# Columns of weights taken two abreast at the start of each group of products, in a hybrid RWKV-7 and neighbourhood-attention trunk on one core

## The chip, the cores and the metric

The kernel runs on one core of one Trainium2 chip. Its time is the device time of one execution in microseconds (us); a comparison takes the median of several runs. PE is the tensor engine, DVE the vector engine, ACT the scalar engine, POOL GpSimd, SP the engine that issues most DMAs. Each engine works through its own queue strictly in the order in which the program wrote it: an instruction that waits holds up everything behind it on its engine.

## The reference

Two requests of 512 tokens by 1024 features pass through two layers with shared weights. Layer 0 is RWKV-7 time mixing with a forward and a backward scan; layer 1 is neighbourhood attention on a grid. Cut to what matters here:

```python
xx = 0.5 * (x_prev + x_next) - xn
lerp = lambda j: xn + xx * mu[j]
r = heads(lerp(0) @ w_r); k = heads(lerp(1) @ w_k); v = heads(lerp(2) @ w_v)
z = xn @ w_z
...                       # decay, a, kk from small products of lerp(3..6)
s = s * w_t + sa b_t + v_t k_t ;  y_t = s r_t      # scan over t, for both directions
out = norm(y) * silu(z);  h = out @ w_o;  x = x + rms_norm(h)
proj = rms_norm(x) @ w_in + b_in                   # layer 1: q, k, v, z
...                       # attention in 8 x 16 windows, gate, w_o, norm, residual
```

All of it is float32. A large product is made of three passes in a faster rounded format: both factors are split into a high and a low half, and high x high, high x low and low x high are added up in one PSUM bank.

## The kernel before, in words

A *column* is 128 output features of one weight matrix: 24 matmuls of 128x512, three for each of eight slices k of the 1024 input features (`gemm`, L430 to L432; in the scan `products`, L826 to L828). A column needs its weights, two halves of 512 wide, each fetched (`raw`), cast to the high half on ACT (`whi`, L379 or L745) and subtracted to the low half on DVE (`wlo`, L380 or L747). It also needs the operands x of its group: eight pairs of tiles `act`, again a cast on ACT (L379 or L771) and a subtraction on DVE (L380 or L773). All columns of one matrix and one request share the operands and form a *group*.

**Before the scan** the work is written as ordinary code and a list scheduler sets the order of each engine. The columns of z for request 0 (z0 to z7) are followed by those of k (k0 to k7). They accumulate in the two PSUM banks called `zy`. A finished z column is taken out of its bank by DVE (L643), a finished k column by ACT (L657, L666). The work on request 1 (`prelude(1)`) runs alongside: squares of x summed on DVE (L445), a sum over features on PE (L458), a square root on ACT (L463), a reciprocal and a diagonal matrix on DVE (L465, L468), its spread on PE (L472). The products L565 to L567 of the small decay matrices follow, and L670 sums the squares of a finished k column.

**In the scan** there are 64 steps in eight blocks of eight: a block is a pair of column groups of one request. A planner (`weave`) writes the queues of PE, DVE and ACT itself, from estimated costs. It holds a set of threads: the scan's steps (first in rank), `preps` and `inverse`, which prepare a block's small matrices, `finish` for its end, and `flow`, which works off nine groups of columns as fill: r and v of request 0, k, r, v and six columns of z of request 1, w_o of request 0, the last two columns of z, then 24 columns of w_in (its operands are made by DVE from the end of layer 0, L795 and L797). Products have the last rank: they fill the time in which PE waits for the scan. Where the planner sees PE idle and cooling down, it writes a filler matmul into a spare bank (L1643). The banks are: two for `pf`, one for `us`, two for `zy`, and three for `pm`. The three `pm` banks hold the columns in work, the columns that wait to be taken out (`posts`), and the small products of `preps` (L896 and L897, taken out by ACT at L900), `inverse` (L1049, L1051), `finish` (L1302, L1312) and the transposes of v (L704, taken out by L707).

Weights live in four pairs of half-column buffers (`NW`), raw weights in three, operands in eighteen `act` tiles, that is nine pairs for groups that need eight. So the next group's operands can be made only as the current group's last column gives its own up, one by one.

**After the scan** (w_o, attention, the second request's w_in) nothing of this applies.

Of the kernel before, what the change touches and what calls it, by code (L numbers as in the profile page):

```python
# [19 lines left out]
P = 128  # L20
# [3 lines left out]
NP = 8  # L24
# [207 lines left out]
class Trunk:  # L232
# [10 lines left out]
    LAST = ("pg", "pg", "po", "pm")  # L243
    PG, PT, NK, NPT = 2, 2, 2, 3
    AHEAD, AHEADW, SCAN_A, SCAN_W = 0, 0, 300, 300
    NAB, NX, NR, NY, NSB, NBI = 2, 2, 2, 2, 4, 2
# [385 lines left out]
    def column(self, s, kind, p, ps):  # L632
# [29 lines left out]
        if kind == "k":  # L662
# [15 lines left out]
            if p == NP - 1:  # L678
                yield "S", None, lambda c: c.at([sp["ss", s].tensor.name])
# [33 lines left out]

    def columns(self, s, kind, x, ps=range(NP)):
        for p in ps:
            w = self.first.pop() if self.first else self.weight(self.a["w_" + kind][p])
            ps = yield from self.gemm(w, x, self.gt)
            for _ in self.column(s, kind, p, ps):
                pass
            yield  # L720

    def flow(self):
# [8 lines left out]
        for k, t in enumerate(self.groups[0][1]):  # L731
            x[0, k] = t

        def loads():
            for c, (_, _, src, _) in enumerate(cols):
                for j in range(2):
                    yield "S", lambda: did["load"] < did["split"] + self.NRAW
                    raw[2 * c + j] = self.load(self.t("raw", (P, self.WP), self.NRAW), src[:, j * self.WP:(j + 1) * self.WP])
                    did["load"] += 1

        def splits():
            for h in range(2 * len(cols)):
                yield "A", lambda: h < did["load"] and h < did["k"] // 4 + self.NW, lambda c: c.at(name(raw[h]))
                hi, lo = (self.t(tag, (P, self.WP), self.NW, F32R) for tag in ("whi", "wlo"))
# [69 lines left out]
        def products():  # L814
            free, room = self.bank()
            for c, (g, j, _, done) in enumerate(cols):
                for k in range(KT):
                    h = 2 * c + k // 4
                    at = slice(k % 4 * P, k % 4 * P + P)
                    yield (  # L820
                        "P", lambda: h in w and (g, k) in x and (k > 0 or (free() and c - 2 not in self.post)),
                        lambda c: max(c.at(name(*w[h], *x[g, k])), 0.0 if k else room(c)))
                    if k == 0:
                        ps = self.p("pm")
                    (hi, lo), (xh, xl) = w[h], x[g, k]
                    nc.tensor.matmul(ps, hi[:, at], xh, start=(k == 0), stop=False)  # L826
                    nc.tensor.matmul(ps, hi[:, at], xl, start=False, stop=False)  # L827
                    nc.tensor.matmul(ps, lo[:, at], xh, start=False, stop=(k == KT - 1))  # L828
                    did["k"] += 1
                    if j == len(self.groups[g][2]) - 1:  # L830
                        did["x"] += 1
                self.post[c] = done(ps)

        def posts(a):
            for c in range(a, len(cols), 2):
# [491 lines left out]
    def out0s(self, s, p, ps):  # L1327
# [14 lines left out]
        else:  # L1342
# [3 lines left out]
            nc.vector.tensor_tensor(self.h_acc, sq, self.h_acc, op=ALU.add)  # L1346
        if p == NP - 1:
            self.made.add(("h", s))
# [309 lines left out]
    def scan_phase(self, mid):  # L1658
# [27 lines left out]
        def fetch():  # L1686
            for q in qs:
                st = self.steps[q]
                yield (
                    "S", lambda: did["states"] >= q - 1 and did["preps"] > st.n and ("v", st.s, 2 * st.pb + 1) in self.made,  # L1690
                    lambda c: c.at([self.sp["ab", st.s, st.pb].tensor.name]))
# [22 lines left out]
        def finish():  # L1714
            for n, (s, pb) in enumerate(self.todo):
                yield "S", lambda: did["steps"] >= NCH * (n + 1) and ("z", s, 2 * pb + 1) in self.sp
                yield from self.finish(s, pb, self.steps[NCH * n].y)
# [16 lines left out]
    def run(self):  # L1734
# [74 lines left out]
class Step:  # L1809
# [122 lines left out]
```

## Time and profile before

| what | value |
|---|---|
| median of 3 runs | 1655.09 us (1649.51 to 1655.29) |
| profiled execution, its own time | 1656.04 us |
| its span in the profile | 1654.2 us |
| PE, DVE, ACT busy | 1558.4, 1220.0, 1014.5 us |
| mean granted PE clock | 0.977 |
| first and last product of the scan's `flow` (L826) | 168.3 and 1159.6 us |

The profiled execution took 0.95 us more than the median, and 1.84 us more than its span. Matmuls overlap in the pipeline: a 128x512 matmul is shown for 0.39 us while the next starts 0.23 us after it, so PE's busy time counts some of it twice where it is dense. A wait in brackets behind a row is the idle time of the engine before that instruction, with what ended it.

### The profile page before, as it was taken

What the parts mean: (1) busy time and instruction counts of PE and PEld (TensorE: products, weight loads), DVE (VectorE), ACT (ScalarE), POOL (GpSimd) and SP (SyncE); (2) the same over time, 40 slices, a digit from 0 to 9 for tenths busy, and PEclk for the clock granted to TensorE, in tenths of its full rate; (3) what the DMA queues carried; (4) which work ended last, traced back from release to release, by engine and by line L of the source; (5) the groups of instructions that cost most, each with busy time, mean ns of one, the idle gap of its engine ahead of it and who ended that gap; (6) DMA issues with size and microseconds to landing.
All of it is one profiled execution on the core that took longest, in us unless ns stands there. A gap on an engine that the chain in (4) does not pass through costs nothing.

```text
span 1654.2 us, 46534 instructions
## 1 busy us (share of the span) xinstructions
PE 1558.4 (94%) x18826; PEld 1195.2 (72%) x18826; DVE 1220.0 (74%) x2711; ACT 1014.5 (61%) x2027; POOL 178.2 (11%) x338
## 2 busy tenths in 40 slices
PE   7989899898989998999888999999999999999998
PEld 6867667676767776766666777777777788777776
DVE  8886669588778786897788897855576685665564
ACT  6577655766755767566475665454567665455562
POOL 0000213311101133100000011000000002100000
PEclk9989999899999999999997999999999999999999
DMA  6455678666677687675776674554864346745553
GB/s 212 158 176 185 183 270 279 217 227 227 206 246 255 201 279 261 201 252 165 226 229 225 199 255 166 179 190 127 276 222 164 109 140 213 244 157 175 169 159 107
DMA packets 176184, 336.29 MB, mean 203 GB/s; under 512 B 20928, under 2 KB 53824, under 8 KB 175968
## 3 DMA queue, kind: packets, MB, share of 16 engines
q1 hardware_dynamic: 152480, 253.07, 47.7%
q0 software_dynamic: 23488, 80.23, 13.8%
q8 instruction: 148, 2.42, 0.6%
q14 instruction: 68, 0.56, 0.1%
HBM read 227.71 MB, written 105.51 MB: 201 GB/s over the span
## 4 chain that ended last, share of the span: by engine, by line
PE 48%; DVE 7%; ACT 5%; DMA 3%; issue 3%; POOL 0%; SPq 0%; DVEq 0%; ACTq 0%; POOLq 0%
PE pg L430 6%; PE pg L431 6%; PE pg L432 6%; PE pm L826 4%; PE pm L827 3%; PE pm L828 3%; PE pf L1114 2%; PE sc L1452 2%; PE po L1485 2%; PE pt L1470 2%; PE us L1233 1%; PE zy L1186 1%; PE us L1213 1%; PE zy L1237 1%; DMA v<-dv 1%
## 5 line engine op out<-in xcount | busy, mean ns | idle before, releaser
L826 PE MATMUL pm<-act,whi 128*128 128x512 f32 x640 | 283.9, 444 | 7.8 <-ACT act L795 3.2
L827 PE MATMUL pm<-act,whi 128*128 128x512 f32 x640 | 257.2, 402 | 10.8 <-DVE act L773 10.1
L828 PE MATMUL pm<-act,wlo 128*128 128x512 f32 x640 | 256.2, 400 | 5.5 <-DVE wlo L747 5.5
L430 PE MATMUL pg<-act,whi 128*128 128x512 f32 x384 | 158.4, 412 | 0.4 <-DVE tmp L1408 0.4
L826 PEld LDWEIGHTS pm<-act,whi 128*128 128x128 f32 x640 | 121.7, 190 | 50.9 <-issue 10.7
L379 ACT CAST whi<-raw 128x512 fp32r<-128x512 f32 x148 | 91.4, 617 | 107.7 <-PE pg L431 66.1
L432 PE MATMUL pg<-act,wlo 128*128 128x512 f32 x384 | 152.5, 397 | 0.0
L431 PE MATMUL pg<-act,whi 128*128 128x512 f32 x384 | 152.4, 397 | 0.0
L827 PEld LDWEIGHTS pm<-act,whi 128*128 128x128 f32 x640 | 122.8, 192 | 36.7 <-DVE act L773 15.9
L828 PEld LDWEIGHTS pm<-act,wlo 128*128 128x128 f32 x640 | 122.7, 192 | 35.5 <-DVE wlo L747 8.9
L380 DVE TENSOR_TENSOR wlo<-raw,whi 128x512 fp32r<-128x512 f32 x148 | 101.3, 686 | 61.1 <-ACT whi L379 60.3
L747 DVE TENSOR_TENSOR wlo<-raw,whi 128x512 fp32r<-128x512 f32 x160 | 108.9, 683 | 33.3 <-ACT whi L745 33.1
L745 ACT CAST whi<-raw 128x512 fp32r<-128x512 f32 x160 | 97.8, 617 | 44.6 <-PE pm L827 23.3
L430 PEld LDWEIGHTS pg<-act,whi 128*128 128x128 f32 x384 | 72.2, 188 | 15.5 <-issue 3.3
L432 PEld LDWEIGHTS pg<-act,wlo 128*128 128x128 f32 x384 | 72.2, 188 | 14.9 <-issue 0.3
L431 PEld LDWEIGHTS pg<-act,whi 128*128 128x128 f32 x384 | 72.4, 189 | 14.1 <-issue 2.5
L1018 DVE TENSOR_TENSOR etmp<-N 128x30 f32<-128x30 f32 (+14 forms) x240 | 78.4, 327 | 4.3
L1020 DVE TENSOR_TENSOR N<-etmp,N 128x30 f32<-128x30 f32 (+14 forms) x240 | 78.5, 327 | 4.0
L1463 DVE CUSTOM_DVE_ANT_0 sb<-sc,bias 128x256 f32<-128x256 f32 x128 | 49.2, 418 | 26.2 <-PE pt L1470 20.1
L1466 ACT ACTIVATE sb<-sb,mx 128x256 f32<-128x256 f32 x128 | 64.1, 502 | 6.9 <-DVE mx L1465 6.6
L1114 PE MATMUL pf<-cab 64*64 64x128 f32 (+1 forms) x2048 | 67.0, 268 | 0.3 <-PE zy L1092 0.3
L1137 DVE TENSOR_TENSOR AK<-zy,cc 128x256 f32<-128x256 f32 x63 | 26.6, 422 | 53.0 <-PE zy L1092 52.5
(409 smaller groups left out, 3686.8 us busy)
## 6 DMA issues: line engine op xcount, KB each, us to landing
dab<-ab POOLq DMA_DIRECT2D x32, 1024.0 KB, 7.0
cab<-dab SPq DMA_DIRECT2D x64, 512.0 KB, 5.0
raw<-in_w_in_dram SPq DMA_DIRECT2D x128, 256.0 KB, 2.9
bias<-in_rpb_dram SPq DMA_DIRECT2D x32, 384.0 KB, 5.2
raw<-in_w_z_dram SPq DMA_DIRECT2D x32, 256.0 KB, 3.6
raw<-in_w_k_dram SPq DMA_DIRECT2D x32, 256.0 KB, 3.0
raw<-in_w_r_dram SPq DMA_DIRECT2D x32, 256.0 KB, 4.2
k<-dk SPq DMA_DIRECT2D x32, 256.0 KB, 4.6
```

The lines of the kernel that those rows point to most:

```text
L379: self.nc.scalar.copy(hi, src)
L380: (eng or self.nc.vector).tensor_tensor(lo, src, hi.bitcast(F32), op=ALU.subtract)
L430: nc.tensor.matmul(ps, hi, x[k][0], start=(k == 0), stop=False)
L431: nc.tensor.matmul(ps, hi, x[k][1], start=False, stop=False)
L432: self.mm = nc.tensor.matmul(ps, lo, x[k][0], start=False, stop=(k == KT - 1))
L745: nc.scalar.copy(hi, raw[h])
L747: nc.vector.tensor_tensor(lo, raw.pop(h), hi.bitcast(F32), op=ALU.subtract)
L826: nc.tensor.matmul(ps, hi[:, at], xh, start=(k == 0), stop=False)
L827: nc.tensor.matmul(ps, hi[:, at], xl, start=False, stop=False)
L828: nc.tensor.matmul(ps, lo[:, at], xh, start=False, stop=(k == KT - 1))
L1020: vt.tensor_tensor(N[:, q + 1:, :q], tv, N[:, q + 1:, :q], op=ALU.add)
L1114: end = nc.tensor.matmul(st.f[half(a), h, 0, d, g] if st.last else st.f[half(a), h, :, d, g], ab[half(h), d, g, 2 * e[d] + 1 - a], rt if s ...
```

## The change

In the scan, the first two columns of every group except the first (`PAIRS`) are worked abreast: slice k of the one, slice k of the other, then slice k + 1. Each operand that arrives now serves six matmuls at once. The order of loads and splits of weight halves follows the order of use, and a buffer is free again when its half has been used four times. The ends of columns are worked by three threads in place of two, so a pair's two ends can be open beside a third. The last two columns (`ENDS`) could be paired too; that list is empty. Since ends may come out of order now, four gates wait for all of a set of tiles in place of the last one. Before the scan, z6 and z7 are written as a pair, and k0 and k1.

```diff
+    PAIRS, ENDS = (1,2,3,4,5,6,7,8), ()
...
-    def columns(self, s, kind, x, ps=range(NP)):
+    def columns(self, s, kind, x, ps=range(NP), two=()):
         for p in ps:
-            w = self.first.pop() if self.first else self.weight(self.a["w_" + kind][p])
-            ps = yield from self.gemm(w, x, self.gt)
-            for _ in self.column(s, kind, p, ps):
-                pass
-            yield
+            if p - 1 in two:
+                continue
+            pair = (p, p + 1) if p in two else (p,)
+            made = [self.gemm(self.first.pop() if self.first else self.weight(self.a["w_" + kind][q]), x, self.gt) for q in pair]
+            outs = yield from abreast(made)
+            for q, ps in zip(pair, outs):
+                for _ in self.column(s, kind, q, ps):
+                    pass
+                yield
...
+            two = [a for a, gs in ((0, self.PAIRS), (n - 2, self.ENDS)) if g in gs]
+            if j in two:
+                turns += [(c + e, k) for k in range(KT) for e in range(2)]
+            elif j - 1 not in two:
+                turns += [(c, k) for k in range(KT)]
+        halves = [2 * c + k // 4 for c, k in turns if k % 4 == 0]
...
-                yield "A", lambda: h < did["load"] and h < did["k"] // 4 + self.NW, lambda c: c.at(name(raw[h]))
+                yield "A", lambda: n < did["load"] and (n < self.NW or used[halves[n - self.NW]] == 4), lambda c: c.at(name(raw[h]))
...
-            for c, (g, j, _, done) in enumerate(cols):
-                for k in range(KT):
+            for c, k in turns:
...
-                        "P", lambda: h in w and (g, k) in x and (k > 0 or (free() and c - 2 not in self.post)),
+                    "P", lambda: h in w and (g, k) in x and (k > 0 or (free() and c - 3 not in self.post)),
...
-            Thread(lambda: 9, products()), Thread(lambda: 2, posts(0)), Thread(lambda: 2, posts(1))]
+            Thread(lambda: 9, products()), *(Thread(lambda: 2, posts(a)) for a in range(3))]
...
-        run(self.columns(0, "z", self.xz), (a, 1))
-        run(self.columns(0, "k", self.shifted(0, 1)), (a, 1))
+        run(self.columns(0, "z", self.xz, two=(6,)), (a, 1))
+        run(self.columns(0, "k", self.shifted(0, 1), two=(0,)), (a, 1))
...
+def abreast(gens):
+    out = [None] * len(gens)
+    todo = list(enumerate(gens))
+    while todo:
+        for n, g in list(todo):
+            try:
+                next(g)
+            except StopIteration as end:
+                out[n] = end.value
+                todo.remove((n, g))
+                continue
+            yield
+    return out
```

How the instructions stand is shown at three places. In the order of the changed kernel the line numbers are shifted: L431 to L433 are the old L430 to L432, L459 and L473 the old L458 and L472, L644 the old L643, L845 to L847 the old L826 to L828, L1665 the old L1643.

First, PE's queue at the join of z and k before the scan. Before, z7 (zy_836) is followed at once by k0 (zy_970):

```order
L430 MATMUL zy_836<-act_140,whi_832 128x512
L431 MATMUL zy_836<-act_139,whi_832 128x512
L432 MATMUL zy_836<-act_140,wlo_833 128x512
L430 MATMUL zy_970<-act_906,whi_962 128x512
L431 MATMUL zy_970<-act_905,whi_962 128x512
L432 MATMUL zy_970<-act_906,wlo_963 128x512
```

Now (z6 is zy_749, z7 is zy_758, k0 is zy_982):

```order
L433 MATMUL zy_749<-act_140,wlo_734 128x512
L431 MATMUL zy_758<-act_140,whi_745 128x512
L432 MATMUL zy_758<-act_139,whi_745 128x512
L433 MATMUL zy_758<-act_140,wlo_746 128x512
L459 MATMUL pm_849<-ones,acc_786 128x1 x4
L473 MATMUL pm_862<-tmp_857,ones 128x128 x4
L431 MATMUL zy_982<-act_906,whi_962 128x512
L432 MATMUL zy_982<-act_905,whi_962 128x512
```

The norm's two small products of request 1, which stood inside and behind k0, now stand ahead of it. The scheduler left z6 all but one matmul ahead of z7, and k0 wholly ahead of k1: the pairs written there are hardly abreast in the queue.

Second, DVE's queue where z6 is taken out of its bank. Before (zy_737 is z6) it is the 115th row of the queue, in the middle of the norm's sums:

```order
L380 TENSOR_TENSOR wlo_963<-raw_958,whi_962 128x512
L445 TENSOR_TENSOR acc_773<-tmp_806,acc_773 128x512
L643 TENSOR_TENSOR tmp_812<-zy_737,vs_158 128x512
L584 SCALAR_TENSOR_TENSOR lm_650<-lr_651,lm_650 128x512
L380 TENSOR_TENSOR wlo_967<-raw_960,whi_966 128x512
```

Now (zy_749 is z6, zy_758 z7) it is the 137th, behind the norm's reciprocal and diagonal; z7's follows as the 142nd, where before it was the 145th:

```order
L466 RECIPROCAL rs_854<-rs_854 128x4
L617 SCALAR_TENSOR_TENSOR xr_951<-xx_415,dv,xr_951 128x512
L469 TENSOR_SCALAR tmp_857<-cc,rs_854 128x128 x4
L644 TENSOR_TENSOR tmp_886<-zy_749,vs_158 128x512
L617 SCALAR_TENSOR_TENSOR xr_1668<-xx_360,dv,xr_1668 128x512
L612 TENSOR_TENSOR h_138_667<-lr_651,h_138_667 64x512
L617 SCALAR_TENSOR_TENSOR xr_1675<-xx_372,dv,xr_1675 128x512
L381 TENSOR_TENSOR act_954<-xr_951,act_955 128x512
L644 TENSOR_TENSOR tmp_894<-zy_758,vs_158 128x512
```

The bank that k0 needs is free only after that row.

Third, PE's queue in the scan at the start of the last group (w_in), ahead of the sixth block. Before, one column (pm_12277) starts, with fillers (L1643) and the inverse's products (L1049) between its slices:

```order
L826 MATMUL pm_12277<-act_12240,whi_12170 128x512
L827 MATMUL pm_12277<-act_12239,whi_12170 128x512
L828 MATMUL pm_12277<-act_12240,wlo_12171 128x512
L1643 MATMUL zy_11763<-cc 128x256
L1049 MATMUL pm_12289<-NA_12254,Go_8993 32x32 x32
L1643 MATMUL zy_11763<-cc 128x256 x3
```

Now two columns (pm_12263 and pm_12274) stand abreast:

```order
L1665 MATMUL zy_11824<-cc 128x256 x5
L845 MATMUL pm_12263<-act_12256,whi_12150 128x512
L846 MATMUL pm_12263<-act_12255,whi_12150 128x512
L847 MATMUL pm_12263<-act_12256,wlo_12151 128x512
L845 MATMUL pm_12274<-act_12256,whi_12192 128x512
L846 MATMUL pm_12274<-act_12255,whi_12192 128x512
L847 MATMUL pm_12274<-act_12256,wlo_12193 128x512
L1665 MATMUL zy_11824<-cc 128x256 x8
L845 MATMUL pm_12263<-act_12300,whi_12150 128x512
```

Each operand serves two columns, and there are more fillers at this place than before. Over the whole program the fillers are 101 before and 103 now. No other count of instructions changes but ACT's loads of its function table, which fall by two. From the last steps of the scan to the end, all queues read alike.

More of the change, by code (lines that the diff above doesn't have):

```diff
@@ L678, in column @@
             if p == NP - 1:
-                yield "S", None, lambda c: c.at([sp["ss", s].tensor.name])
+                yield "S", lambda: all(("k", s, q) in self.made for q in range(NP)), lambda c: c.at([sp["ss", s].tensor.name])
                 rn = self.tmp((P, 64))
@@ L815, in products @@
             free, room = self.bank()
[L816 to L832 removed]
+            out = {}
+            for c, k in turns:
+                g, j, _, done = cols[c]
+                h = 2 * c + k // 4
+                at = slice(k % 4 * P, k % 4 * P + P)
+                yield (
+                    "P", lambda: h in w and (g, k) in x and (k > 0 or (free() and c - 3 not in self.post)),
+                    lambda c: max(c.at(name(*w[h], *x[g, k])), 0.0 if k else room(c)))
+                if k == 0:
+                    out[c] = self.p("pm")
+                ps = out[c]
+                (hi, lo), (xh, xl) = w[h], x[g, k]
+                nc.tensor.matmul(ps, hi[:, at], xh, start=(k == 0), stop=False)
+                nc.tensor.matmul(ps, hi[:, at], xl, start=False, stop=False)
+                nc.tensor.matmul(ps, lo[:, at], xh, start=False, stop=(k == KT - 1))
+                did["k"] += 1
+                used[h] += 1
+                if j == len(self.groups[g][2]) - 1:
+                    did["x"] += 1
+                if k == KT - 1:
+                    self.post[c] = done(out.pop(c))
         def posts(a):
[L835 removed]
+            for c in range(a, len(cols), 3):
                 yield "A", lambda: c in self.post
@@ L1689, in fetch @@
                 yield (
-                    "S", lambda: did["states"] >= q - 1 and did["preps"] > st.n and ("v", st.s, 2 * st.pb + 1) in self.made,
+                    "S", lambda: did["states"] >= q - 1 and did["preps"] > st.n and all(("v", st.s, 2 * st.pb + g) in self.made for g in range(2)),
                     lambda c: c.at([self.sp["ab", st.s, st.pb].tensor.name]))
@@ L1715, in finish @@
             for n, (s, pb) in enumerate(self.todo):
-                yield "S", lambda: did["steps"] >= NCH * (n + 1) and ("z", s, 2 * pb + 1) in self.sp
+                yield "S", lambda: did["steps"] >= NCH * (n + 1) and all(("z", s, 2 * pb + g) in self.sp for g in range(2))
                 yield from self.finish(s, pb, self.steps[NCH * n].y)
```

20 lines of the change are left out of this document (13 added, 7 removed).

## The prediction

> **What bounds the kernel now.** I read the page's first two parts, then the stretches of time, then PE's waits inside the scan, and last the order of time at the join of z and k.
>
> ```profile
> span 1654.2 us, 46534 instructions
> ...
> PE 1558.4 (94%) x18826; PEld 1195.2 (72%) x18826; DVE 1220.0 (74%) x2711; ACT 1014.5 (61%) x2027; POOL 178.2 (11%) x338
> ...
> core 0: us, PE busy (x) PEld busy (x) DVE busy (x) ACT busy (x) POOL busy (x), PEclk, DMA share, GB/s
> 62.00:84.00 22.00, 21.00 (x94) 17.05 (x92) 20.84 (x34) 16.72 (x30) 0.24 (x4) 1.00 0.34 115
> 84.00:96.00 12.00, 8.77 (x29) 6.48 (x29) 11.84 (x23) 10.52 (x17) 0.02 (x1) 0.57 0.18 54
> 96.00:142.00 46.00, 46.00 (x188) 32.99 (x187) 32.02 (x49) 28.98 (x49) 0.00 (x0) 1.00 0.64 221
> 142.00:168.00 26.00, 26.00 (x106) 18.49 (x105) 18.78 (x29) 20.82 (x36) 0.00 (x0) 1.00 0.49 168
> 168.00:1165.00 997.00, 928.19 (x15467) 703.24 (x15466) 777.89 (x1495) 620.98 (x1205) 145.80 (x240) 0.97 0.68 219
> 1165.00:1654.20 489.20, 475.57 (x2728) 374.75 (x2726) 305.26 (x962) 279.60 (x634) 30.63 (x57) 1.00 0.54 178
> ```
>
> PE bounds nearly all of it. From 96 to 168 us it has no gap at all, so whatever PE loses ahead of 96 us arrives whole at the scan. From 84 to 96 DVE is the bound (11.84 of 12.00 us busy) and PE runs at a granted clock of 0.57. In the scan, 168 to 1165 us, PE is idle for 997.00 - 928.19 = 68.8 us, and some of its busy time is filler:
>
> ```profile
> L1643 PE MATMUL zy<-cc 128*128 128x256 f32 x202 | 54.5, 401 | 1.0 <-ACT Z L1198 0.5 <-ACT y L1252 0.5
> PE pm L827 <- DVE act L773: 10.1, 11, 4.7
> PE pm L828 <- DVE wlo L747: 5.5, 6, 2.5
> PE pm L826 <- ACT act L795: 3.2, 2, 2.3
> PE pm L704 <- ACT vs L707: 1.6, 1, 1.6
> PE pm L826 <- ACT vs L707: 1.1, 1, 1.1
> ```
>
> So the scan has 68.8 us of idle and 54.5 us of filler, each filler two rows of the 202. Its slack is no single wait. The largest, 10.1 us, is what the change aims at: a product that waits for the low half of its group's next operand. L795 is the same for the last group. Waits for weights are 5.5 us, and waits for a `pm` bank (PE released by an ACT copy out of it) are a few us.
>
> **The change part by part: before the scan.** These are the rows at the join.
>
> ```profile
> 71.16 0.69 DVE L650 SCALAR_TENSOR_TENSOR tmp<-tmp,tmp 128x512 f32<-128x512 f32 x1 [0.45 <-ACT tmp L647]
> 83.98 0.51 PE L430 MATMUL zy<-act,whi 128*128 128x512 f32 x1 [1.00 <-ACT act L379]
> 87.56 0.80 PE L431 MATMUL zy<-act,whi 128*128 128x512 f32 x1 [3.08 <-DVE act L380]
> 88.15 0.63 PE L432 MATMUL zy<-act,wlo 128*128 128x512 f32 x1
> 88.58 0.63 PE L430 MATMUL zy<-act,whi 128*128 128x512 f32 x1
> 95.09 0.68 DVE L643 TENSOR_TENSOR tmp<-zy,vs 128x512 f32<-128x512 f32 x1
> 95.94 0.48 PE L430 MATMUL zy<-act,whi 128*128 128x512 f32 x1
> 96.25 0.39 PE L431 MATMUL zy<-act,whi 128*128 128x512 f32 x1
> 96.48 0.39 PE L432 MATMUL zy<-act,wlo 128*128 128x512 f32 x1
> 100.91 1.02 PE L670 MATMUL pm<-tmp,cc 128*2 128x512 f32 x2
> 101.86 0.50 PE L430 MATMUL zy<-act,whi 128*128 128x512 f32 x1
> 103.59 0.39 PE L431 MATMUL zy<-act,whi 128*128 128x512 f32 x1
> ```
>
> k0 runs up to 95.9 us with waits of 1.00 and 3.08 us in it, and slowly: starts lie 88.58 - 88.15 = 0.43 us apart in place of 0.23 (96.48 - 96.25). k1 starts at 95.94, 0.17 us after DVE has emptied z7's bank (95.09 + 0.68 = 95.77): with two banks a column starts when the column two before it is out.
>
> That rule now falls on k0. z6 leaves its bank with DVE's 137th row, where it was the 115th. Where the old queue emptied z7 with its 145th row at 95.09, and took 95.09 - 71.16 = 23.9 us for the 38 rows from the 107th, that is 0.63 us a row, eight rows fewer are 5.0 us. Two waits come in: the low half of k0's second weights now waits for z6's last product, held back behind z7 (about 0.7 us, a row), and the reciprocal waits for the norm's first product and the root, whose sum ends DVE's own part earlier than in the old order (another 0.7, an estimate from the row time). So z6 is out at 95.09 - 5.0 + 1.4 + 0.68 = 92.2, and k0 starts at 92.3. PE meanwhile has only L458 and L472. k0's 24 matmuls, seven at 0.43 and seventeen at 0.23, take 6.9 us; k1 and three products of L565 that stand in it 27 x 0.23 = 6.2: 105.4 us. The old queue had the same work done at 103.59, less L670's 0.95 (101.86 - 100.91) and one matmul of k2, 0.23, which the new queue has still to do: 102.4. The join costs **3.0 us**. Bounds: no new waits and full clock at once give k0 at 90.9 and 0; the slow clock through all of k0 gives 6.4. I take 3.0 because DVE's row rate is measured here over the same kinds of rows. Nothing hides it: PE is full from 96 to 168 us.
>
> The granted clock is the other half of that. The Trainium skill, TensorE: Matmul & The Clock Gate, Part 1, says the array falls to half rate after about 3.4 us of idle and returns after about 3.4 us of sustained work. The rows above agree on the two rates (0.43 and 0.23). By that figure, as an estimate, k0 would open with eight slow matmuls, and the join would cost 3.2 us.
>
> **The scan.** No instruction is added but fillers. They go from 101 to 103: two more at 54.5 / 101 = 0.54 us are **1.1 us**. What remains is which waits go and which come. The operand rate is the point of the change:
>
> ```profile
> L773 DVE TENSOR_TENSOR act<-xr,act 128x512 fp32r<-128x512 f32 x56 | 38.2, 684 | 24.9 <-ACT act L771 24.4 <-PE pm L827 0.4
> L747 DVE TENSOR_TENSOR wlo<-raw,whi 128x512 fp32r<-128x512 f32 x160 | 108.9, 683 | 33.3 <-ACT whi L745 33.1
> ```
>
> One operand takes DVE 0.684 us and feeds three matmuls, 3 x 0.23 = 0.69 us of PE. As DVE is 78% busy in the scan (777.89 of 997.00), it cannot keep that pace in the first column of a group. Abreast, each operand feeds 1.38 us. So the waits on L773 and L795, 10.1 + 3.2 = 13.3 us, should mostly go from where they stand. What is late next is in the order: the columns of a group are used up no slower than before, the blocks of the scan still wait for `preps` and `inverse` on DVE, and the planner writes as many fillers as before, only elsewhere. Ahead of the sixth block there are more. I therefore put the waits that go at 13.3 and the waits that come back at the same, **0 net**. The bounds: -13.3 with the slow clock behind these waits (rival one), and the price of rival two. The half-columns also change: a pair asks for all four weight buffers in its first half, where a column asked for two. That can add to the 5.5 us of L747, and it can be hidden by the 1.38 us per slice; I take 0 of -5.5 to +5.5. The third end thread, the order of raw loads on SP's queue, the gates on all in place of the last, and two ACT table loads fewer have no wait of PE behind them: 0.
>
> **The sum.** 1656.0 (the profiled execution) + 3.0 + 1.1 + 0 = 1660.1. That execution lay 0.95 us above the median, so the forecast is **1659 us**. From the ends of the join (0 to 6.4) and of the weights (5.5 either way), this case alone spans 1651 to 1668.
>
> **Rivals.** *One, faster: the waits do not come back.* These are stretches around the starts of groups:
>
> ```profile
> 234.00:247.00 13.00, 10.96 (x94) 7.78 (x95) 12.29 (x24) 6.18 (x13) 1.57 (x3) 0.74 0.94 318
> 534.00:540.00 6.00, 5.30 (x70) 3.46 (x64) 2.74 (x4) 4.92 (x8) 1.89 (x2) 0.72 0.72 227
> 740.00:760.00 20.00, 15.11 (x233) 11.36 (x231) 14.77 (x27) 7.76 (x13) 2.71 (x4) 0.91 0.66 214
> 850.00:895.00 45.00, 35.59 (x394) 26.71 (x386) 38.06 (x67) 25.93 (x44) 4.44 (x6) 0.80 0.86 284
> ```
>
> The clock is down to 0.74, 0.72, 0.91 and 0.80 there. What that costs is PE's busy time by the missing clock: 10.96 x 0.26 + 5.30 x 0.28 + 15.11 x 0.09 + 35.59 x 0.20 = 12.8 us. I give half, 6.4, to the waits for operands. With 13.3 that is 19.7 us gained: 1656.0 - 19.7 + 3.0 - 0.95 = **1638 us**. For it speaks that these stretches are real and early; against it, the fillers that did not get fewer.
>
> *Two, slower: a pair holds two of the three `pm` banks.* The pair's two banks are held for 48 matmuls, and then both at once until ACT or DVE has emptied them. `preps` and `inverse` are left one bank.
>
> ```profile
> L900 ACT ACTIVATE th<-pm,dv 128x512 f32<-128x512 f32 x64 | 43.9, 685 | 7.8 <-PE pm L897 7.5
> L896 PE MATMUL pm<-h,w2h 128*128 128x512 f32 x64 | 28.7, 449 | 1.1 <-ACT tmp L673 0.4 <-ACT vs L476 0.3 <-ACT NA L1056 0.3
> L897 PE MATMUL pm<-h,w2l 128*128 128x512 f32 x64 | 25.6, 400 | 4.5 <-DVE w2l L882 4.4
> ```
>
> Eight tiles of `preps` per block each need two matmuls and a tanh. With two banks the matmuls of one run under the tanh of another; with one they follow each other, 0.449 + 0.400 = 0.85 us more per tile, 6.8 a block. It decides where a block waits for `preps` with the columns used up: the orders show fillers ahead of the fourth, fifth and sixth block. Three blocks cost 20.4 us: 1656.0 + 3.0 + 20.4 - 0.95 = **1678 us**. Against it: waits on banks are small now (1.6 and 1.1 us in the rows above). Perfetto Trace Analysis of the Trainium skill (Optimizing Tensor Performance, Matmuls) asks that independent groups rotate through different banks so that emptying one overlaps the next one's matmuls; two columns that end together are against it. No row of the kernel before shows a pair.
>
> *Three, the join as meant.* If k0's operands come early enough, the 1.00 and 3.08 us and the slow clock (8.77 x 0.43 = 3.8 us) go: 1656.0 - 7.9 - 0.95 = **1647 us**. Against it stands the order, which pushes z6's bank behind the norm and leaves the columns nearly one after the other. The pair of k is then a change that does not do what it says.
>
> **How the numbers follow.** A measurement of this kernel can tell about 0.5%, 8.3 us, from no change. The forecast has 0.45, rival one 0.23, rival two 0.22, rival three 0.10. The forecast's own span crosses 1663 us at its upper end and touches the lower bound of no change hardly: I count 0.28 of it as the same, 0.14 as slower, 0.03 as faster. Rival one gives 0.21 faster and 0.02 same; two 0.21 slower, 0.01 same; three 0.02 faster, 0.08 same. Together faster 0.26, same 0.39, slower 0.35. The range reaches to both ends, 1636 to 1681: the upper and lower tails of rivals one and two, a fifth in all, lie outside.
>
> **What would show it.** Right: DVE's L644 for z6 near 91.5 us and k0 at 92.3, k1 done near 105, no gap from there to the scan, which starts 3 us late. In the scan PE's waits for L773's tiles fall below 4 us in total, and idle time plus fillers stay within 5 us of 68.8 + 54.5. Rival one: idle time falls by over 10 us and the clock of the scan rises above 0.97. Rival two: new waits of PE on ACT's copies out of `pm`, and blocks four to six start later than the work ahead of them explains. The forecast is wrong if the scan's length moves by over 8 us either way, or if the stretch after it changes from 489 us.

## The result and the profile after

Over 12 runs each the changed kernel took 1665.26 us (median; 1658.85 to 1672.71) against 1655.19 us (1649.51 to 1659.64): a ratio of 1.0062, 95% interval 1.0046 to 1.0078. It is 10 us slower, and 6 us above the forecast of 1659, inside the range (1636 to 1681). Its profiled execution took 1661.72 us, 3.5 below its median, so it shows only 5.7 of the 10 us.

The page of the kernel after: its span, the busy times, and the group of fillers.

```profile
span 1660.0 us, 46526 instructions
...
PE 1550.4 (93%) x18830; PEld 1189.3 (72%) x18830; DVE 1221.0 (74%) x2711; ACT 1012.3 (61%) x2025; POOL 177.8 (11%) x338
...
L1665 PE MATMUL zy<-cc 128*128 128x256 f32 x206 | 51.9, 391 | 0.0
```

All that follows rests on one sum. The span is PE's idle time, plus its time in fillers, plus its time in its own matmuls. Without fillers there are 18,624 matmuls in both kernels (18,826 - 202 and 18,830 - 206), so a change in their own time is no change of work. It is a change of speed, and in part of how closely the matmuls follow one another, since each is shown for longer than it keeps the next one waiting. Overlap is counted once: from 96 to 142 us before, 188 matmuls of some 0.39 us each (some 73 us if added up) give 46.00 us busy of 46.00. Before: 1654.2 = 95.8 idle + 54.5 fillers + 1503.9 own. After: 1660.0 = 109.6 + 51.9 + 1498.5. Idle time grew by 13.8 us, fillers fell by 2.6 and own time by 5.4.

The same stretches of time after, with the columns as before:

```profile
core 0: us, PE busy (x) PEld busy (x) DVE busy (x) ACT busy (x) POOL busy (x), PEclk, DMA share, GB/s
62.00:84.00 22.00, 18.73 (x83) 15.16 (x81) 20.46 (x33) 16.26 (x29) 0.26 (x4) 1.00 0.30 96
84.00:96.00 12.00, 7.70 (x29) 6.89 (x30) 11.73 (x23) 10.52 (x17) 0.00 (x0) 0.57 0.13 45
...
142.00:168.00 26.00, 25.50 (x104) 18.59 (x104) 16.48 (x26) 18.82 (x32) 0.00 (x0) 1.00 0.43 150
168.00:1165.00 997.00, 918.58 (x15454) 695.12 (x15455) 777.86 (x1494) 618.65 (x1204) 145.24 (x239) 0.98 0.68 219
```

From 62 to 96 us PE is idle for 7.6 us, where it was 4.2; from 142 to 168 it has half a microsecond of gap. The scan's idle time in the fixed stretch rises from 68.8 to 78.4 us, and its clock from 0.97 to 0.98.

The join, in PE's order of time:

```profile
84.99 1.84 PE L459 MATMUL pm<-ones,acc 128*128 128x1 f32 x8 [4.27 <-DVE acc L446]
90.14 2.04 PE L473 MATMUL pm<-tmp,ones 128*128 128x128 f32 x8 [3.31 <-DVE tmp L469]
91.83 0.77 PE L431 MATMUL zy<-act,whi 128*128 128x512 f32 x1
...
94.11 0.47 PE L433 MATMUL zy<-act,wlo 128*128 128x512 f32 x1
94.42 0.39 PE L431 MATMUL zy<-act,whi 128*128 128x512 f32 x1
...
104.79 1.02 PE L671 MATMUL pm<-tmp,cc 128*2 128x512 f32 x2
...
172.22 0.58 PE L845 MATMUL pm<-act,whi 128*128 128x512 f32 x1
```

And DVE's row that empties z6's bank:

```profile
90.50 0.69 DVE L644 TENSOR_TENSOR tmp<-zy,vs 128x512 f32<-128x512 f32 x1
```

k0 starts at 91.83, 0.64 us after z6 is out (90.50 + 0.69 = 91.19), and without a gap behind the rows of L473 (90.14 to 92.18). So the bank was free by then: what ended last is the norm's own products, which now stand ahead of k0 in PE's queue and wait for DVE, L459 4.27 us for the sum of squares and L473 3.31 us for the diagonal. These two waits are all of PE's 7.6 us of idle time from 62 to 96. k1 and the three products of L565 are done by 104.79, and the scan's first product starts at 172.22, 3.9 us later than the 168.3 before.

PE's waits inside the scan:

```profile
PE pm L845 <- ACT act L788: 9.2, 1, 9.2
PE pm L847 <- DVE wlo L764: 6.1, 7, 2.2
...
PE pm L846 <- DVE act L814: 3.4, 8, 1.3
PE pm L845 <- ACT act L812: 3.3, 6, 1.1
PE pm L917 <- ACT th L921: 3.0, 5, 1.0
...
PE pm L1323 <- ACT th L921: 2.1, 1, 2.1
...
PE pm L705 <- ACT th L921: 1.2, 2, 0.8
...
PE pm L846 <- DVE act L790: 1.0, 2, 0.8
```

The wait at which the change aimed, for DVE's half of an operand (L773, now L790), fell from 10.1 us in 11 places to 1.0 in 2. But ACT's half of an operand (L788, the old L771) now costs 9.2 us in one place, where it cost 0.2. This is how it comes about: a row of the chain of waits, then one of DVE and one of ACT.

```profile
742.13 11.24 DMA dab<-ab
...
753.50 0.69 DVE L961 TENSOR_TENSOR ab<-r,e 128x512 f32<-128x512 f32 x1 [6.13 <-DMA dab<-ab]
...
755.67 0.81 ACT L973 ACTIVATE pp<-th,dv 128x512 f32<-128x512 f32 x1 [7.52 <-DVE ab L961]
```

The row of PE that ends the wait:

```profile
757.05 0.80 PE L845 MATMUL pm<-act,whi 128*128 128x512 f32 x1 [9.21 <-ACT act L788]
```

A store of 1 MB from POOL's queue (`preps` of the next block) takes 11.24 us. DVE's next write into the same buffer waits 6.13 us for it, ACT's `pp` stands behind that DVE row, and the cast of the first operand of w_o behind `pp`. PE has run dry by then.

### The profile page after: what moved, and what is told of

The parts are those of the page before. It is cut to its first block, busy times and chain, and to the rows that moved or that the text cites. A ratio compares the mean times of both kernels' runs of the same rounds, so it can differ in the third digit from the quotient of the medians.

```text
span 1660.0 us, 46526 instructions
## 1 busy us (share of the span) xinstructions
PE 1550.4 (93%) x18830; PEld 1189.3 (72%) x18830; DVE 1221.0 (74%) x2711; ACT 1012.3 (61%) x2025; POOL 177.8 (11%) x338
## 4 chain that ended last, share of the span: by engine, by line
PE 64%; ACT 11%; DVE 10%; DMA 10%; issue 4%; SPq 0%; POOL 0%; DVEq 0%; ACTq 0%; POOLq 0%
PE pg L431 6%; PE pm L845 6%; PE pg L432 6%; PE pg L433 6%; PE pm L847 4%; PE pm L846 4%; DMA dab<-ab 3%; PE pf L1135 2%; PE us L1254 2%; PE sc L1474 2%; PE po L1507 2%; PE zy L1207 2%; PE us L1234 2%; PE pt L1492 2%; PE zy L432 2%
## 5 line engine op out<-in xcount | busy, mean ns | idle before, releaser
L845 PE MATMUL pm<-act,whi 128*128 128x512 f32 x640 | 282.8, 442 | 19.3 <-ACT act L788 9.2
L847 PE MATMUL pm<-act,wlo 128*128 128x512 f32 x640 | 255.7, 400 | 6.1 <-DVE wlo L764 6.1
L845 PEld LDWEIGHTS pm<-act,whi 128*128 128x128 f32 x640 | 122.4, 191 | 65.6 <-issue 16.4
L431 PE MATMUL pg<-act,whi 128*128 128x512 f32 x384 | 158.4, 413 | 0.4 <-DVE tmp L1430 0.4
L433 PE MATMUL pg<-act,wlo 128*128 128x512 f32 x384 | 152.4, 397 | 0.0
L432 PE MATMUL pg<-act,whi 128*128 128x512 f32 x384 | 152.4, 397 | 0.0
L847 PEld LDWEIGHTS pm<-act,wlo 128*128 128x128 f32 x640 | 122.6, 192 | 36.8 <-DVE wlo L764 9.4
L431 PEld LDWEIGHTS pg<-act,whi 128*128 128x128 f32 x384 | 72.3, 188 | 15.5 <-issue 3.3
L433 PEld LDWEIGHTS pg<-act,wlo 128*128 128x128 f32 x384 | 72.2, 188 | 14.9 <-issue 0.3
L432 PEld LDWEIGHTS pg<-act,whi 128*128 128x128 f32 x384 | 72.4, 189 | 14.0 <-issue 2.5
L1246 ACT COPY X<-us 64x256 f32<-64x256 f32 x128 | 46.9, 366 | 36.0 <-PE zy L1113 33.8
```

The costliest lines, as they stand in the source:

```text
L431: nc.tensor.matmul(ps, hi, x[k][0], start=(k == 0), stop=False)
L432: nc.tensor.matmul(ps, hi, x[k][1], start=False, stop=False)
L433: self.mm = nc.tensor.matmul(ps, lo, x[k][0], start=False, stop=(k == KT - 1))
```

## The experiments

The first theory was that the pairs cost the time. After the first four runs three others stood: T (the third end thread, or its wider window, is the cost), F (time goes by the number of fillers) and P (the kernel before is one written order out of many, and any edit to the planner draws another). All were compared with the kernel before on the same chip, in five rounds. e1 to e4 ran on one chip, e5 to e8 on a second and e9 to e12 on a third; the kernel before took 1654.3, 1654.9 and 1655.2 us there.

**One part at a time.** Four kernels were made from the changed one. e1 has neither pairs in the scan nor the pairs of z and k, and keeps the third end thread, the buffer rule and the gates:

```diff
-    PAIRS, ENDS = (1,2,3,4,5,6,7,8), ()
+    PAIRS, ENDS = (), ()
...
-        run(self.columns(0, "z", self.xz, two=(6,)), (a, 1))
-        run(self.columns(0, "k", self.shifted(0, 1), two=(0,)), (a, 1))
+        run(self.columns(0, "z", self.xz), (a, 1))
+        run(self.columns(0, "k", self.shifted(0, 1)), (a, 1))
```

> The changed kernel with no pair at all: three end threads, the new buffer rule and the new gates stay. Theory (the pairs cost the time: 3.9 us at the join before the scan and the rest in the scan): within 2 us of the kernel before, 1653 to 1657. Rival (the third end thread and the gates cost it): 1660 to 1665, like the changed kernel. Rival (the planner answers any edit with a few us either way): 1648 to 1662 with no rule.

e2 takes only the second part of this diff (scan pairs stay, no pairs of z and k):

> The changed kernel without the pairs of z and k before the scan; the scan's pairs stay. Theory: the join's 3.9 us come back, 1661 against 1665, and the first product of the scan starts at 168.3 again in place of 172.2. Rival (the scan hides the start): no change, 1665.

e3 takes only its first part (pairs of z and k stay, none in the scan):

> The changed kernel with the pairs of z and k before the scan and no pair in the scan. Theory: 3.9 us above the kernel with no pair, so about 1659, and the scan starts near 172. Rival (the scan absorbs the delay, or its own pairs cost all): as the kernel with no pair.

e4 takes the second part and pairs the last group alone, `PAIRS = (8,)`:

> Pairs in the last group (w_in) alone, none before the scan. In the two traces the stretch between the fifth and the seventh block was the one place where the changed kernel gained on the kernel before (19.3 us behind at the fifth block's start, 5.2 us behind at the seventh's). Theory (pairs pay where the group's operands come slowly from DVE): faster than the kernel before by 5 to 11 us, 1644 to 1650. Rival (that stretch only gives back what the transition before it lost): within 3 us of the kernel with no pair.

Measured: e1 1667.20 us (ratio 1.0080, 1.0052 to 1.0108), e2 1662.33 (1.0045, 1.0027 to 1.0062), e3 1667.80 (1.0093, 1.0067 to 1.0119), e4 1678.83 (1.0146, 1.0122 to 1.0170). The first theory falls: with no pair at all the kernel is already 13 us slower. The pairs of the scan bring the medians down, by 4.9 us (e1 to e2) and 2.5 us (e3 to the whole change), though the intervals of each two overlap. The pairs of z and k cost 2.9 us (e2 to the whole change) and 0.6 (e1 to e3). By the trace they move the start of the scan by 3.4 us (168.8 to 172.2) and 3.2 us (170.2 to 173.4). Over all the profiles of this document the scan starts at 168.2 to 170.2 us in the eleven without these pairs and at 171.6 to 173.4 in the three with them. e2 came as expected. e3 was expected 3.9 us above e1 and lies 0.6 above it, within the noise. e4 missed both of its expectations, 1644 to 1650 and within 3 us of e1: it is 11.6 us above e1.

The page of e1, and then its waits of PE in the scan:

```profile
span 1668.1 us, 46549 instructions
...
PE 1571.8 (94%) x18834; PEld 1204.3 (72%) x18834; DVE 1223.0 (73%) x2711; ACT 1012.6 (61%) x2025; POOL 177.8 (11%) x338
...
L1665 PE MATMUL zy<-cc 128*128 128x256 f32 x210 | 56.7, 412 | 0.0
```

```profile
PE pm L846 <- DVE act L790: 18.3, 14, 3.2
PE pm L918 <- DVE w2l L903: 10.3, 4, 5.6
```

By the sum, e1 has 96.3 us of idle time and 56.7 of fillers, nearly as before, but 1515.1 us of own time for the same 18,624 matmuls: 11.2 us more. Nearly all of that is the clock, 0.970 over the whole where it was 0.977 (10.6 us of it, worked out as told below the table). e2, with the pairs back:

```profile
span 1660.5 us, 46524 instructions
...
PE 1555.0 (94%) x18830; PEld 1192.7 (72%) x18830; DVE 1219.7 (73%) x2711; ACT 1011.2 (61%) x2025; POOL 177.9 (11%) x338
...
L1665 PE MATMUL zy<-cc 128*128 128x256 f32 x206 | 51.4, 388 | 0.0
```

```profile
PE pm L845 <- ACT act L788: 8.6, 1, 8.6
...
PE pm L847 <- DVE wlo L764: 4.9, 6, 2.4
...
PE pm L918 <- DVE w2l L903: 3.2, 1, 3.2
...
PE pm L846 <- DVE act L790: 1.2, 3, 0.8
```

Its own time is back at 1503.6, but idle time has gone up to 105.5. So the pairs do what they were written for (L790 from 18.3 us to 1.2; L918's wait for `w2l` falls too, from 10.3 to 3.2) and the clock returns (0.979), but other waits of PE come in that are longer by 9.2 us in all than those that went. The largest is the cast of L788 again, 8.6 us.

**Which half of the third end thread.** e5 keeps the scan's pairs and goes back to two threads and the window of two columns (a column may start once the one two before it has been taken out); e6 has no pairs, three threads and the window of two; e7 no pairs, two threads and the window of three. e8 is the kernel before with one number of the planner changed that means nothing for the work. The window, undone in e5 (made from e2) and e6 (from e1):

```diff
-                    "P", lambda: h in w and (g, k) in x and (k > 0 or (free() and c - 3 not in self.post)),
+                    "P", lambda: h in w and (g, k) in x and (k > 0 or (free() and c - 2 not in self.post)),
```

The threads, undone in e5 and in e7 (from e1):

```diff
-            for c in range(a, len(cols), 3):
+            for c in range(a, len(cols), 2):
...
-            Thread(lambda: 9, products()), *(Thread(lambda: 2, posts(a)) for a in range(3))]
+            Thread(lambda: 9, products()), *(Thread(lambda: 2, posts(a)) for a in range(2))]
```

The planner's tie in e8:

```diff
-    NZ1, STOCK, EPS, NEAR = 6, 1, 60.0, 400.0
+    NZ1, STOCK, EPS, NEAR = 6, 1, 70.0, 400.0
```

> The scan's eight pairs as in e2, but columns' ends in two threads and the window two columns wide, as in the kernel before; no pairs of z and k. Theory T (the third end thread with its wider window costs about 13 us, as e1 against the kernel before, and the pairs give back 5, as e2 against e1): 1654 - 5 = 1649 us. Rival P (the third thread has no cost of its own; a change of one entry reshuffles the written order by so much, and e1 was one draw): as likely above 1654 as below, and no reason for 1649. Rival F (time goes with the fillers that the order holds, 101, 105, 103, 113 for 1654, 1667, 1662, 1679 us, some 2 us each): this order holds 94, so 1640 to 1646. In all three PE's waits on the operands' subtraction stay below 4 us, as in e2.

> No pairs at all; three end threads, but a column may start only when the column two before it has been taken by its end thread, as in the kernel before. Against e1 only the window is undone. Theory T in its first form (the third thread itself is the cost): 1667 us, as e1. T in its second form (the wider window is the cost): 1654 us. Rival P: anywhere within 15 us of 1660. Rival F (92 fillers in this order): about 1638 to 1645.

> No pairs; two end threads as in the kernel before, but a column may start as soon as the column three before it has been taken. Against the kernel before only the window is changed. T in its first form (third thread): 1654 us. T in its second form (window): 1667 us. Rival P: anywhere within 15 us of 1660. Rival F (78 fillers, the fewest of all orders): 1610 to 1630 us.

> The kernel before with one number of the planner changed: threads whose ready times lie within 70 ns of each other count as tied, in place of 60. No pairs, two threads, window two. It means nothing for the work, and writes another order in the scan. Theory T says nothing against 1654 us: within 3 us of it. Rival P: off by 5 us or more to either side. Rival F (122 fillers): 1680 us or more.

Measured: e5 1665.28 us (1.0069, 1.0044 to 1.0095), e6 1662.85 (1.0049, 1.0028 to 1.0071), e7 1649.48 (0.9973, 0.9956 to 0.9989), e8 1677.26 (1.0145, 1.0116 to 1.0175). T in its simple form fails at e5: without the third thread the pairs are no faster than with it. T's second form, in which the wider window is the cost, fails at e7, and e6 lies between the 1654 and 1667 us of T's two forms. F fails at e5 and e6, whose 94 and 92 fillers should have given 1638 to 1646, and at e7, whose 78 should have given 1610 to 1630. e8 is what P asks for: a neutral edit costs 22 us. And e7 is the fastest of all, 5.4 us below the kernel before.

The page of e7, and of e5:

```profile
span 1646.9 us, 46414 instructions
...
PE 1544.2 (94%) x18780; PEld 1183.0 (72%) x18780; DVE 1219.1 (74%) x2711; ACT 1014.5 (62%) x2027; POOL 177.9 (11%) x338
...
L1665 PE MATMUL zy<-cc 128*128 128x256 f32 x156 | 42.8, 414 | 0.5 <-ACT Z L1219 0.5
```

```profile
span 1666.1 us, 46512 instructions
...
PE 1550.7 (93%) x18812; PEld 1189.8 (71%) x18812; DVE 1221.9 (73%) x2711; ACT 1012.9 (61%) x2025; POOL 177.9 (11%) x338
...
L1665 PE MATMUL zy<-cc 128*128 128x256 f32 x188 | 47.9, 388 | 1.1 <-ACT Z L1219 1.1
```

e7 stands against the kernel before with 11.7 us less of fillers, 2.5 less of own time and 6.9 more of idle time. e5 shows the pairs without the third thread: own time 1502.8, 1.1 us less than before, at a mean clock of 0.981 where it was 0.977; but idle time is 115.4 us, 19.6 more. The long wait behind the store isn't what makes it so: waits for L788 are 2.2 us in e5.

**A second draw.** To part P from T, four kernels were written once more with the planner's tie at 80 ns: the kernel before (e9), e1 (e10), the whole change (e11), and e7 (e12). The edit is that of e8 with 80.0.

> The kernel before with the planner's tie at 80 ns in place of 60: a second neutral edit, for a second written order of the same kernel. Theory P (the kernel before at 60 is one order out of a spread some 25 us wide, 1649 to 1677 so far): 1660 to 1675, as e8. Rival T (the orders differ little and e8 was an outlier; the change costs): within 4 us of 1654. The order holds 104 fillers, so by fillers alone about 1659.

> e1 (three end threads with the wider window, no pairs) with the tie at 80 ns. Against e9 it has only the third thread. Theory T (the third thread costs PE about 11 us of its own busy time, at a granted clock of 0.95 to 0.97 in the scan, in e1, e3, e4 and e6 alike): 10 to 13 us above e9, clock of the scan at 0.96, PE's own products in the scan at 880 us or more. Theory P (no cost of its own): within 8 us of e9 on either side, and the clock as in e9.

> The whole change (pairs in the scan and at the join, three end threads) with the tie at 80 ns. Theory P with pairs that trade waits and clock against other idle time, as e1 to e2 did: operands' waits below 5 us, PE's own products near 868 us, idle time near 80 us; with only 80 fillers in this order the time is 1652 to 1660. If pairs had a net gain or loss of their own in every order, it would lie as far from e9 as the change lay from the kernel before: 10 us above e9. The join's 3 us stay: the first product of the scan near 172.

> e7 (two end threads, window three columns wide, no pairs) with the tie at 80 ns. If the wider window with two threads is a gain of its own, it lies 5 us or more below e9, as e7 below the kernel before. Theory P: no such order among the two is to be expected, 1655 to 1670 whatever e9 gives; the order holds 99 fillers.

Measured: e9 1668.27 us (1.0087, 1.0069 to 1.0105), e10 1673.39 (1.0112, 1.0095 to 1.0130), e11 1671.80 (1.0105, 1.0082 to 1.0128), e12 1661.15 (1.0037, 1.0018 to 1.0056). e9 came as P expected. e10 lies 5.1 us above e9: inside the 8 us of P, and short of the 10 to 13 of T. e12 lies 7.1 below e9, which the window's own gain and P both allow. The whole change lies 3.5 us above its own kernel before here, not 10, and its interval overlaps e9's. e11 was missed: 1652 to 1660 was expected, 1671.8 came, with 80 fillers, which ends F. Its waits show the price of pairs in another place than before, at the weights (6.1 us in the longest):

```profile
PE pm L847 <- DVE wlo L764: 16.6, 8, 6.1
...
PE pm L846 <- DVE act L790: 3.5, 5, 1.9
```

All fourteen orders, by the sum (span less PE's busy time, the fillers' group, and PE's busy time less that; one profiled execution each, in us; the clock is the mean over all runs of the kernel):

| kernel | end threads, window, pairs | median | idle | fillers | own | clock |
|---|---|---|---|---|---|---|
| before | 2, 2, none | 1655.2 | 95.8 | 54.5 | 1503.9 | 0.977 |
| e8, e9 (tie 70, 80) | 2, 2, none | 1677.3, 1668.3 | 106.0, 105.7 | 66.3, 56.4 | 1501.2, 1502.9 | 0.978, 0.976 |
| e7, e12 (60, 80) | 2, 3, none | 1649.5, 1661.2 | 102.7, 103.4 | 42.8, 50.2 | 1501.4, 1503.9 | 0.980, 0.981 |
| e6 | 3, 2, none | 1662.9 | 102.4 | 51.0 | 1512.3 | 0.972 |
| e1, e10 (60, 80) | 3, 3, none | 1667.2, 1673.4 | 96.3, 101.4 | 56.7, 55.5 | 1515.1, 1511.6 | 0.972, 0.975 |
| e3 | 3, 3, z and k | 1667.8 | 97.8 | 54.6 | 1511.1 | 0.972 |
| e4 | 3, 3, last group | 1678.8 | 106.5 | 58.7 | 1512.3 | 0.972 |
| e2 | 3, 3, scan | 1662.3 | 105.5 | 51.4 | 1503.6 | 0.980 |
| after, e11 (60, 80) | 3, 3, all | 1665.3, 1671.8 | 109.6, 115.5 | 51.9, 43.4 | 1498.5, 1509.0 | 0.980, 0.974 |
| e5 | 2, 2, scan | 1665.3 | 115.4 | 47.9 | 1502.8 | 0.979 |

Own time mixes the clock with how closely matmuls follow one another. The clock's part can be worked out from the clock records of the same traces, as own busy time times the share of the clock that was not granted, moment by moment. It is 30.1 us before; 21.6 to 30.1 in all six orders with two threads; 33.3 to 42.7 in the five with three threads and no pairs, or only those of the join or of the last group; and 26.6, 21.6 and 32.1 in e2, after and e11. What is left of own time varies from 1469.5 to 1482.2 us, so a few microseconds of own time say nothing of the clock.

Three things can be read across the draws, but none as a time, since two neutral edits put the kernel before 13 and 22 us higher.

*Three end threads go with a lower clock where the scan is not paired throughout.* Own time is 1501 to 1504 us in the six orders with two threads, and 1511 to 1515 in the five named above; the mean clock of all runs is 0.976 to 0.981 against 0.972 to 0.975. (e6's profile is its slowest execution, 1667.42 us, at 0.968, so its 1512.3 is high.) The three comparisons that change only the number of threads are slower by 8 us (before to e6), 17.7 (e7 to e1) and 12.2 (e12 to e10). Against it stands e9 to e10, with the window changed too: 8.7 us more own time, but a clock of 0.976 and 0.975, and only 5.1 us.

*Orders with the scan's pairs have more idle time*: 105.5 to 115.5 us in all four, 95.8 to 106.5 in the other ten. From e1 to e2 it is +9.2 us, from e3 to after +11.8, from e10 to e11 +14.1 (there with the join's pairs), from before to e5 +19.6; the neutral edits alone gave +10.2 and +9.9. What comes back is own time and fillers: 11.5 + 5.3 us from e1 to e2, 2.6 + 12.1 from e10 to e11.

*The wider window with two threads is ahead in both draws*, by 5.4 us at tie 60 and 7.1 at tie 80.

And there is P as well: the kernel before is the lowest of its three draws, by its idle time of 95.8 us. So of the 10 us only the join's 3 have a cause that the traces show. The rest is less than a neutral edit does, and at tie 80, where the whole change costs 3.5 us, hardly anything of it is left.

Why the clock is lower with three end threads is not settled; no run took the cause apart further. Nor was the store's wait taken away: its 9 us have a cause that is read from the rows, and that was not tried.

## Why the prediction was right, and where it was not

**The join: right in size, with another wait at its end.** z6's row was expected near 91.5 and stands at 90.50; k0 at 92.3, found 91.83; k1 done at 105.4, found 104.79. Expected +3.0 us at the start of the scan, found +3.9 in the profile of after, 3.2 and 3.4 in the comparisons that change nothing else. But k0 was to start when z6's bank comes free. The bank was free 0.64 us earlier, and k0 stood behind L473 in PE's queue. Both waited for the same stretch of DVE's queue (L469, then L644), so the size came out; an earlier row for z6 alone would not have moved k0. The clock is as the rows said: k0 opens with six slow matmuls (91.83 to 94.11, (94.11 - 91.83) / 5 = 0.46 us apart), where seven were charged. Rival three (the join as meant) is out, since the slow clock and the idle time stayed.

**The third end thread: the step that failed.** It was put at 0, because "no wait of PE" stood behind it. What the runs show in its place is not a wait but a lower clock: 7.7 to 13.7 us more own time in the three comparisons above (8.4, with e6's slowest execution, 13.7 and 7.7; the clock's part of it rose by 12.6, 18.7 and 11.7). The medians rose by 8 to 18 us, of which each new order has its unknown part. The threads are part of what the planner orders by, so the question was how the whole order moves and not who waits for a thread. The other terms put at 0 with it were right: without pairs, with two threads and the window of two, the queues of the changed kernel read as those before, so the gates and the buffer rule do nothing by themselves.

**The waits that come back: put too low, and made up by the clock.** The prediction took out 13.3 us and put 13.3 back. In the scan idle time rose by 9.6 us, so more came back than went; own time and fillers fell by 8.0 over the whole kernel, and only with these is the net near 0. The waits on DVE's operand halves went (L790: 1.0 us), under the 4 us named. Of w_in's operands the prediction let 3.2 us go, read as waits on a low half. The row names ACT's half (L795, now L812), and it stayed, at 3.3; DVE's half (L797, now L814) rose to 3.4 from this:

```profile
PE pm L827 <- DVE act L797: 0.6, 2, 0.4
```

The ACT half of the other operands (L788), which the sum did not have, took 9.2 us. "The blocks still wait" was the argument; what the trace shows is one long wait behind a store and many small ones. The other half was not foreseen: the pairs, next to three threads, lower own time (by 11.5 and 12.6 us at tie 60, only 2.6 at 80).

**Fillers.** Two more were to cost 1.1 us. Two more came, but their group took 51.9 in place of 54.5 us: a row is shown for 391 ns in place of 401. How much of that is the clock was not worked out. The sign was wrong, and the size off by 3.7 us.

**Weights.** 0 of a span of -5.5 to +5.5: the wait went from 5.5 to 6.1 us. In e11 it was 16.6, so the span was too narrow for another order.

**The sum.** 1660.1 was expected of a profiled execution and 1661.7 came. That closeness is partly luck: by medians the third thread and its window (+12.9, e1), the scan's pairs (-4.9, e2 to e1) and the join (+2.9) make 10.9, and 10.1 was measured; the prediction had 0, 0 and 3.0 for these, and 1.1 for fillers. (These three steps lead from the kernel before to the changed one, so that they add up is no check.) Of the 6.3 us by which the median lies above the forecast, 3.5 is the distance of this profile from its own median, the reverse of the 0.95 that was taken off.

**The rivals.** One (the waits do not come back) is out: idle time in the scan rose by 9.6 us. Own time fell by 5.4 us where 6.4 was put for it, but that need not be its mechanism: e5, with the same pairs and two threads, has 1.1 us less than before, and the neutral e8 2.7 less. Two (a pair holds two of three `pm` banks) exists, at a fifth of its price: PE's waits for ACT to take `th` out of a bank are the rows of L921 above, 3.0 + 2.1 + 1.2 = 6.3 us. Before they were 2.4 (L900 is now L921), so 3.9 us are new, where 20.4 were put:

```profile
PE pm L1302 <- ACT th L900: 1.7, 2, 1.3
...
PE pm L704 <- ACT th L900: 0.7, 1, 0.7
```

Its other sign, late blocks, is there: the first product of L1254 (the old L1233) of the fourth, fifth and sixth block starts 5.2, 20.2 and 14.6 us later. For the fifth (785.6 us in place of 765.4) no bank is needed: 30 more matmuls of columns stand ahead of it (1155 against 1125, at 0.23 us 6.9 us), the join costs 3.9 and the wait behind the store 9.2, together 20.0; 22 filler rows fewer stand against that, and other small waits were not added up. Rival three is told with the join. Of the signs that were named, two failed: idle time plus fillers was to stay within 5 us of 68.8 + 54.5 = 123.3, and it is 78.4 + 51.9 = 130.3; and no gap was to lie ahead of the scan, where there is one of 0.5 us. The scan's length from first to last product (991.8 us before, 994.0 after) and the stretch behind it (494.1 and 493.8) stayed within their bounds.

## What to carry to other kernels

Where a planner writes the queues, every change of a number in its rules draws a new order, and a neutral edit has to be measured before an edit's few microseconds are read as its effect; here the neutral ones moved the kernel by 13 and 22 us. Split the bound engine's span into idle time, filler and own time at a fixed count of instructions: it helps to tell a slow clock from a wait, which a list of waits cannot. That nothing waits for a thread does not make it free to change the number of threads. The fastest version found here (e7, two end threads with the window of three and no pairs, 0.9973, 0.9956 to 0.9989) kept one line of the change and left out the rest; it is one draw, and with another tie (e12) the same kernel took 1661 us.

## What the runs showed of the hardware

PE's granted clock can stay low while PE is shown busy without a gap. In e1, in four stretches of 5 us, with the columns as before:

```profile
655.00:660.00 5.00, 3.44 (x73) 2.64 (x74) 3.53 (x5) 4.88 (x11) 0.43 (x1) 0.84 0.22 82
660.00:665.00 5.00, 5.00 (x73) 3.61 (x72) 3.38 (x6) 4.44 (x8) 3.31 (x6) 0.50 0.53 142
665.00:670.00 5.00, 5.00 (x134) 3.92 (x132) 1.54 (x2) 3.60 (x7) 0.00 (x0) 0.50 0.97 345
670.00:675.00 5.00, 5.00 (x86) 3.85 (x75) 2.42 (x5) 4.62 (x12) 0.00 (x0) 0.77 0.48 151
```

The order of time inside it:

```profile
662.00 1.92 PE L1072 MATMUL pm<-MT,NA 32*32 32x32 f32 x64
...
667.13 1.92 PE L1072 MATMUL pm<-MT,NA 32*32 32x32 f32 x64
668.98 1.19 PE L996 MATMUL pf<-ab 64*32 64x64 f32 x64
670.09 0.79 PE L845 MATMUL pm<-act,whi 128*128 128x512 f32 x1
...
672.35 0.39 PE L847 MATMUL pm<-act,wlo 128*128 128x512 f32 x1
```

For ten microseconds PE is shown full and its clock at half; the fast rows begin at 672.35, 2.3 us after the last of the 32x32 and 64x64 products gave way to one of 128x512 (670.09). The Trainium skill, TensorE: Matmul & The Clock Gate, Part 1, has the clock come back after about 3.4 us of sustained work. The join is near it: k0 is fast 2.6 us after its own start (94.42 - 91.83) and 4.3 us after PE's idle time ended (94.42 - 90.14). This stretch is not near it. One reading is that small tiles don't count as work; no run tried it.
